# Seven products in place of eight for two output blocks of the last MLP's last pass, and a unit-wise activation in MLP 1

## The chip, the cores and the metric

The kernel runs on one core of a Trainium2 chip. The metric is device time in microseconds, the median of three runs. A core has TensorE (PE, matrix products into PSUM; PEld is its weight load), VectorE (DVE), ScalarE (ACT), GpSimd (POOL) and SyncE (SP, which issues the transfers from memory). Each engine works off its own queue of instructions in order.

## The reference

One sequence of 256 positions, width 2048, two layers: a short gated convolution with an MLP, then latent attention with an MLP. Behind each of the four sub-layers stands a normalisation of `ALPHA * x + f(x)`. The change is in the two MLPs:

```python
D_MODEL = 2048; SEQ = 256; D_FF = 4 * D_MODEL
ALPHA = (2 * DEPTH) ** 0.25

def sq_relu_mlp(x, w1, w2):
    return jnp.square(jax.nn.relu(x @ w1)) @ w2

h = layer_norm(ALPHA * h + mix, ln_g[layer, 0], ln_b[layer, 0])
h = layer_norm(ALPHA * h + sq_relu_mlp(h, mlp_w1[layer], mlp_w2[layer]), ln_g[layer, 1], ln_b[layer, 1])
```

All is float32.

## The kernel before, in words

*Two halves for each operand.* A float32 operand is split into a high part in a reduced format and a low part (`split`, L134: ScalarE casts the high part, L136, and VectorE subtracts it, L137). A product is then three matmuls: high by high, high by low, low by high. Weights come raw from memory in pieces of 128 x 1024 (512 KB, `load_raw`), and are split like this. `take` (L192) hands out the pieces in the order of the list `stream`, and has those prepared that lie up to five steps ahead. There are seven buffers for raw pieces and nine pairs for split ones.

*An MLP* (`mlp`, L586; `idx` 1 is MLP 1, `idx` 3 the last MLP) has 8192 hidden columns in eight passes (`q`, 0 to 7) of eight units (`m`, 0 to 7) of 128. A unit is a product with `w1`: 16 pairs of matmuls (`mm_run`, L230), a 512-wide one with the high part (L224) and a 256-wide one with the low part (L228). `turned=2` swaps the two at the third pair; `TURN` (L41) says for which units. The result is brought out of PSUM by `whole` (L363: ScalarE copies one half, L366, VectorE adds the other, L367), goes through relu and square (L732), and is split into `h` (tiles h1c, h1a in MLP 1; h3c, h3a in the last MLP). Two neighbouring units form a pair, and share one tile `u`.

*The way down.* The second product with `w2` has four output blocks of 512 columns, for two halves `t` of 128 rows each. In passes 0 and 7 it is done plainly (`down`, L324, `dot`, L306): for each block, half and unit three matmuls 512 wide. In passes 1 to 6 (`FAST`) two blocks at a time (`g` 0 or 1: blocks 0 and 1, or 2 and 3) take a pair of units as a 2 x 2 problem, by seven products in place of eight (`fast_products`, L356; `FACTORS`, L351). For that `form` (L641) makes three sums out of the pair, the pair's split grows to 896 columns, and a piece of `w2f` is prepared by `prepare` with three more sums (L171, L175, L178), three splits of 1024 and one of 512. The seven running results stand in seven PSUM banks; where the pair of blocks changes, they are put back (`put_back`, L620) into `acc` and `sums`, and the next are fetched (`resume`, L693). At the end `fold` (L622) adds them up, eight sums of 512 for each `g`, three or two behind each unit of pass 7. Products stand five units behind their own (`SHIFT`): pass 7 begins with products of pass 6.

*The end of MLP 1.* Pass 7's pair of units 6 and 7 goes through relu, square and split together. Then the four blocks follow by `down` in `to_wide` (L767). The residual, parked in memory, is fetched into the place of `sums` by POOL (L763), and VectorE scales it (L419).

*The end of the last MLP.* Pass 7's units 5 to 7 have no products between them. `last_sum` (L633) copies the folded blocks back into PSUM banks, `to_out` (L1026) adds all four blocks of pass 7 plainly on top: blocks 0 and 1 by `down`, then blocks 2 and 3 by `down_late`, half `t` = 0 ahead of `t` = 1. `finished` (L1041) takes statistics of each block (L1042), multiplies by the gain (L1045, for `t` = 1), and with the last block of a half normalises and stores: by VectorE for `t` = 0 (L1056, L1059), and for `t` = 1 partly by four matmuls (L1071, L1076) and a last step on ScalarE (L1080). The gains and offsets `gbt` are fetched in the place of the units' input, so behind the last unit.

*Order.* Within what the data allow a scheduler sets the order of each engine's queue when the kernel is built. `tc.issue_after(ins)` puts the instructions made inside it behind `ins` on `ins`'s engine.

The lines at the place of the stream that change:

```python
def mlp_stream(l):
    out = halves(w1[l, :QC]) + halves(w2[l, 0])
    for q, m, pair in steps():
        out += halves(w1[l, q * QC + m])
        if pair:
            p, i, j, g = pair
            out.append((w2f[l, p, g, j, 0], w2f[l, p, g, j, 1]))
    return out + halves(w2[l, NQ - 1])
```

Of the kernel before, what the change touches and what calls it, by code (L numbers as in the profile page):

```python
# [40 lines left out]
def TURN(q, m, extra):  # L41
    return m == 0 or not (q == 1 and m < SHIFT or q == NQ - 1 and m > SHIFT) or extra and q == 1 and m <= NB
# [14 lines left out]
def trunk(ctx: ExitStack, tc: tile.TileContext, xT, vecs, lead, w_first, w_in, w_out, w_kv, w_q, w_uk, w_uv,  # L57
# [31 lines left out]
    def steps():  # L89

        for q in range(1, NQ):
            for m in range(QC):
                p, i = (q, m - SHIFT) if m >= SHIFT else (q - 1, m + QC - SHIFT)
                yield q, m, (p, i // NB, i % NB, (p % 2) ^ (i // NB)) if p in FAST else None

    def mlp_stream(l):
        out = halves(w1[l, :QC]) + halves(w2[l, 0])
        for q, m, pair in steps():
            out += halves(w1[l, q * QC + m])
# [34 lines left out]
    def split(hi, lo, src):  # L134

        nc.scalar.copy(hi, src)  # L136
        nc.vector.tensor_tensor(lo, src, hi.bitcast(F32), ALU.subtract)  # L137
# [218 lines left out]
    def fast_products(ps, x, j, fresh, ready, onto=()):  # L356

        b, = take(1, 6)
        a = {n: [x[j // 2][:, j % 2, o, i * P:(i + 1) * P] for o in range(2)] for i, n in enumerate(LEFT)}
        for p, l, r in FACTORS:  # L360
            dot(ps[p], b[r], a[l], p in fresh, p in ready, onto=p in onto)
# [224 lines left out]
    def mlp(idx, ln, blocks, fast, begin=None, extra=None, last=False):  # L586
# [43 lines left out]

        finals = {}
# [50 lines left out]
        factors = [act.tile([P, QC // 4, 2, 7 * P], F32R, tag=tag, name=f"h{idx}{tag}") for tag in ("c", "a2")]  # L682
# [13 lines left out]
        begun = {0: FAST[0], 1: FAST[0]}  # L696

        def products_of(p, i, j, g):
# [12 lines left out]
            if p == FAST[-1] and j == NB - 1:  # L711
                folds = chain(folds, fold(g))

        for q, m, pair in steps():
# [11 lines left out]
            late = q in FAST and m >= QC - 2  # L726
# [6 lines left out]
            if m % 2 and (m > 1 or lone):  # L733
                finish_pair(m // 2, u)
# [8 lines left out]
            if q == NQ - 1:  # L743
                for _ in range(3 if m >= SHIFT else 2):
                    next(folds, None)
            if pair:
                products_of(*pair)
            if m == 1 and not lone:
                finish_pair(0, u)
# [276 lines left out]
    def to_out(block, finals, h):  # L1026
# [13 lines left out]

        def finished(n, t, ps):  # L1041
            nc.vector.bn_stats(out=stats[:, t, n, :], in_=ps)  # L1042
            if n < NB - 1:
# [18 lines left out]
            if t == 0:  # L1062
                rsqrt(r, ve)
                for i in range(NB):
# [5 lines left out]
            for i in range(n):  # L1070
                nc.tensor.matmul(finals[i, t], means, gbt[:, i, :BW], start=False, stop=i > 0, skip_group_check=True)  # L1071
# [4 lines left out]
            nc.tensor.matmul(finals[0, t], devs, gbt[:, 0, BW:], start=False, stop=True, skip_group_check=True)  # L1076
            scaled(n, us[n], gbt[:, n, BW:])
            for i in range(1, n):
                scaled(i, finals[i, t], gbt[:, i, BW:])
            nc.scalar.activation(block(0, t), finals[0, t], AF.Copy, scale=r)  # L1080
            store(t, 0)
# [102 lines left out]
```

## Time and profile before

| what | value |
|---|---|
| median of three runs | 2000.63 us (2000.51 to 2001.29) |
| the profiled execution's own time | 2002.59 us |
| its span | 2000.7 us |
| granted clock of TensorE, mean | 0.998 |
| moved from memory | 384 MB, 194 GB/s over the span |

In the profile a row of a timeline gives start, duration, engine, line, operation, tiles and shape, and in square brackets the idle time of the engine ahead of it with what ended it; `x2` means two in a row. In a row of a group stand the count, the busy time and the mean duration of one, then the idle time ahead of them. A row of a table of stretches gives from:to and length, then the busy time of each engine with its count of instructions, the granted clock, the share of the transfer engines and their rate. The end of a matmul is modelled, so the step from one matmul's start to the next one's says more than its duration; VectorE, too, starts an instruction a little ahead of the shown end of the one before.

### The profile page before, as it was taken

What the parts mean: (1) busy time and instruction counts of PE and PEld (TensorE: products, weight loads), DVE (VectorE), ACT (ScalarE), POOL (GpSimd) and SP (SyncE); (2) the same over time, 40 slices, a digit from 0 to 9 for tenths busy, and PEclk for the clock granted to TensorE, in tenths of its full rate; (3) what the DMA queues carried; (4) which work ended last, traced back from release to release, by engine and by line L of the source; (5) the groups of instructions that cost most, each with busy time, mean ns of one, the idle gap of its engine ahead of it and who ended that gap; (6) DMA issues with size and microseconds to landing.
All of it is one profiled execution on the core that took longest, in us unless ns stands there. A gap on an engine that the chain in (4) does not pass through costs nothing.

```text
span 2000.7 us, 29698 instructions
## 1 busy us (share of the span) xinstructions
PE 1988.5 (99%) x11062; PEld 1732.5 (87%) x11062; DVE 1720.3 (86%) x2505; ACT 1289.0 (64%) x1914; POOL 5.6 (0%) x27
## 2 busy tenths in 40 slices
PE   9999999999999999999999999999999999999998
PEld 8888888988788888888889998898888888888886
DVE  8667667787899999999988988778889999999995
ACT  6444445586667777677756665558666776767772
POOL 0000000000000000000000000000000000000000
PEclk9999999999999999999999999999999999999999
DMA  9766666574565555665764643656456556565572
GB/s 339 213 190 189 189 189 190 182 238 143 180 215 191 200 194 196 210 205 204 246 223 153 184 144 106 211 182 196 140 194 216 170 203 216 180 212 197 205 267 96
DMA packets 107712, 390.00 MB, mean 195 GB/s; under 512 B 11952, under 2 KB 12720, under 8 KB 107056
## 3 DMA queue, kind: packets, MB, share of 16 engines
q1 hardware_dynamic: 106560, 383.79, 58.7%
q0 software_dynamic: 864, 4.19, 0.6%
q8 instruction: 86, 1.41, 0.3%
q14 instruction: 58, 0.48, 0.1%
q10 hardware_dynamic: 144, 0.13, 0.0%
HBM read 383.87 MB, written 4.19 MB: 194 GB/s over the span
## 4 chain that ended last, share of the span: by engine, by line
PE 95%; DMA 2%; DVE 1%; issue 1%; ACT 0%; SPq 0%; DVEq 0%; POOLq 0%; ACTq 0%
PE ps_u L224 20%; PE ps_l L224 13%; PE ps_u L228 10%; PE ps L312 7%; PE ps L311 7%; PE ps L309 7%; PE ps_l L228 7%; PE ps_d L312 2%; PE ps_d L309 2%; PE ps_d L311 2%; PE ps_w L258 2%; PE ps_w L257 2%; PE ps_w L256 2%; DMA raw<-in_w2f_dram 1%; PE ps_g L258 1%; PE ps_g L256 1%
## 5 line engine op out<-in xcount | busy, mean ns | idle before, releaser
L137 DVE TENSOR_TENSOR lo<-raw,hi 128x1024 fp32r<-128x1024 f32 x710 | 854.6, 1218 | 167.1 <-ACT hi L136 97.6
L136 ACT CAST hi<-raw 128x1024 fp32r<-128x1024 f32 x710 | 732.5, 1054 | 220.2 <-PE ps_l L224 102.2
L224 PE MATMUL ps_u<-xhl,hi 128*128 128x512 f32 x1792 | 621.2, 393 | 0.0
L228 PE MATMUL ps_u<-xhl,lo 128*128 128x256 f32 x1792 | 485.0, 280 | 0.0
L224 PEld LDWEIGHTS ps_u<-xhl,hi 128*128 128x128 f32 x1792 | 328.8, 187 | 67.5 <-DVE fp L367 0.9
L228 PEld LDWEIGHTS ps_u<-xhl,lo 128*128 128x128 f32 x1792 | 338.1, 189 | 12.9
L224 PE MATMUL ps_l<-xhl_a,hi 128*128 128x512 f32 x704 | 244.1, 393 | 0.0
L228 PE MATMUL ps_l<-xhl_a,lo 128*128 128x256 f32 x704 | 195.4, 279 | 0.0
L136 ACT CAST hi_t<-raw_t 128x1024 fp32r<-128x1024 f32 x96 | 101.5, 1057 | 120.4 <-DVE raw_t L171 115.4
L224 PEld LDWEIGHTS ps_l<-xhl_a,hi 128*128 128x128 f32 x704 | 132.1, 188 | 29.9
L228 PEld LDWEIGHTS ps_l<-xhl_a,lo 128*128 128x128 f32 x704 | 131.9, 188 | 0.2
L171 DVE TENSOR_TENSOR raw_t<-raw,raw 128x1024 f32<-128x1024 f32 x96 | 116.9, 1217 | 9.8 <-DMA raw<-in_w2f_dram 9.8
L137 DVE TENSOR_TENSOR lo_t<-raw_t,hi_t 128x1024 fp32r<-128x1024 f32 x96 | 116.9, 1218 | 2.1 <-ACT hi_t L136 1.7
L366 ACT COPY t<-ps_u 128x256 f32<-128x256 f32 x112 | 41.7, 372 | 95.0 <-PE ps_u L228 94.7
L224 PE MATMUL ps_l<-z,hi 128*128 128x512 f32 x240 | 82.4, 391 | 0.0
L258 PE MATMUL ps_w<-xd,hi 128*128 128x258 f32 x256 | 72.7, 284 | 0.0
L256 PE MATMUL ps_w<-xd,hi 128*128 128x258 f32 x256 | 72.3, 282 | 0.0
L257 PE MATMUL ps_w<-xd,lo 128*128 128x258 f32 x256 | 72.3, 282 | 0.0
L224 PE MATMUL ps_l<-oT,hi 128*128 128x512 f32 x208 | 71.3, 391 | 0.0
L732 ACT ACTIVATE fp<-fp 128x512 f32<-128x512 f32 (+1 forms) x112 | 65.9, 588 | 7.2 <-DVE fp L367 6.8
L178 DVE TENSOR_TENSOR raw<-raw 128x512 f32<-128x512 f32 x96 | 66.1, 688 | 2.0
L175 DVE TENSOR_TENSOR raw<-raw,raw_t 128x512 f32<-128x512 f32 x96 | 65.6, 683 | 0.8
(350 smaller groups left out, 3880.0 us busy)
## 6 DMA issues: line engine op xcount, KB each, us to landing
raw<-in_w_dram SPq DMA_DIRECT2D x320, 512.0 KB, 4.1
raw<-in_w2f_dram SPq DMA_DIRECT2D x192, 512.0 KB, 5.2
raw<-in_w_in_dram SPq DMA_DIRECT2D x88, 512.0 KB, 3.7
raw<-in_w_out_dram SPq DMA_DIRECT2D x32, 512.0 KB, 3.7
raw<-in_w_o_dram SPq DMA_DIRECT2D x32, 512.0 KB, 4.2
raw<-in_w_kv_dram SPq DMA_DIRECT2D x10, 512.0 KB, 4.6
raw<-in_w_q_dram SPq DMA_DIRECT2D x8, 512.0 KB, 4.0
raw<-in_w_uk_dram SPq DMA_DIRECT2D x8, 512.0 KB, 4.6
```

What stands on the lines that cost most here:

```text
L136: nc.scalar.copy(hi, src)
L137: nc.vector.tensor_tensor(lo, src, hi.bitcast(F32), ALU.subtract)
L171: nc.vector.tensor_tensor(t.rearrange(two, a=2), b12.unsqueeze(1).to_broadcast([P, 2, BW]), r1.rearrange(two, a=2), ALU.subtract)
L178: nc.vector.tensor_tensor(t4, b21, b12, ALU.subtract)
L224: nc.tensor.matmul(ps, w[blk // 8][0][:, blk % 8, :], x, start=first, stop=False)
L228: nc.tensor.matmul(ps[:, :T], w[blk // 8][1][:, blk % 8, :], x[:, :T], start=False, stop=last)
L256: nc.tensor.matmul(ps[:, :W], hi, x[k][:, :W], start=k == 0, stop=False)
L257: nc.tensor.matmul(ps[:, :W], lo, x[k][:, :W], start=False, stop=False)
L258: nc.tensor.matmul(ps[:, :W], hi, x[k][:, W:], start=False, stop=k == NC - 1)
L309: nc.tensor.matmul(ps, x[0], w[0], start=first, stop=False, skip_group_check=onto)
L311: nc.tensor.matmul(ps[:, at], x[0], w[1][:, at], start=False, stop=False, skip_group_check=onto)
L312: nc.tensor.matmul(ps, x[1], w[0], start=False, stop=last, skip_group_check=onto)
```

## The change

For MLP 1: units 6 and 7 of pass 7 are activated and split each by itself; unit 6's square stays on ScalarE, unit 7's is done on VectorE in one instruction.

For the last MLP: pass 7's output blocks 2 and 3 are done by seven products. `steps` runs past pass 7 for that: the pairs 0 to 3 of pass 7 stand behind its units 5, 6, 7 and at the end. The products go on in the banks in which pass 6 left blocks 2 and 3; behind pair 3 four of the seven results (`OWN`) are put back into `sums`, three stay in PSUM. `last_sum` fetches blocks 0 and 1 alone. `down_late` then does blocks 0 and 1, and behind its first block stand (`between`) the eight sums of `fold_last`, some of them in PSUM, and the statistics of blocks 2 and 3. The order of the blocks in the normalisation is 2, 3, 0, 1. The instructions on VectorE that are made between pair 3's split and the end of the pass stand behind that split (`issue_after`). The factors' tiles grow from seven to eight columns of 128 and hold the pair's plain values, too. `TURN` loses the case for units 1 to 4 of the last MLP's pass 1, which stand behind transposes.

```diff
-def TURN(q, m, extra):
-    return m == 0 or not (q == 1 and m < SHIFT or q == NQ - 1 and m > SHIFT) or extra and q == 1 and m <= NB
+def TURN(q, m):
+    return m == 0 or not (q == 1 and m < SHIFT or q == NQ - 1 and m > SHIFT)
...
-    def steps():
+    def steps(last):
-        for q in range(1, NQ):
-            for m in range(QC):
+        for q in range(1, NQ + 1):
+            for m in range(QC if q < NQ else SHIFT):
                 p, i = (q, m - SHIFT) if m >= SHIFT else (q - 1, m + QC - SHIFT)
-                yield q, m, (p, i // NB, i % NB, (p % 2) ^ (i // NB)) if p in FAST else None
+                pair = (p, i // NB, i % NB, (p % 2) ^ (i // NB)) if p in FAST or last and p == NQ - 1 and i < NB else None
+                if q < NQ or pair:
+                    yield q, m, pair
...
-        return out + halves(w2[l, NQ - 1])
+        return out + halves(w2[l, NQ - 1, :2] if l else w2[l, NQ - 1])
...
-    def down_late(x, put, blocks, sums):
+    def down_late(x, put, blocks, sums, between):
         ws = {}
         for t in range(2):
             for n in blocks:
+                if t == 0 and n != blocks[0]:
+                    between()
...
+        def fold_last(g):
+            s1, s5, s7, s6 = (sums[:, i, g, :] for i in range(4))
+            left, right = 2 * g, 2 * g + 1
+            finals.update({(left, 1): ps["2"], (right, 1): ps["3"], (left, 0): ps["4"], (right, 0): block(right, 0)})
+            for d, a, b in ((ps["2"], ps["2"], s1), (s6, s6, s1), (ps["3"], ps["3"], s6), (s7, s7, s6),
+                            (ps["4"], ps["4"], s7), (block(right, 0), block(right, 0), s7), (ps["3"], ps["3"], s5),
+                            (block(right, 0), block(right, 0), s5)):
+                nc.vector.tensor_tensor(d, a, b, ALU.add)
...
         def finish_pair(j, u):
             f = factors[j // 2][:, j % 2]
-            if q in FAST:
+            if q in FAST or last:
                 form(u)
-                split(f[:, 0, :], f[:, 1, :], u[:, P:])
+                at = slice(P if q in FAST else 0, 8 * P)
             else:
-                split(f[:, 0, :2 * T], f[:, 1, :2 * T], u[:, :2 * T])
+                at = slice(0, 2 * T)
+            return split(f[:, 0, at], f[:, 1, at], u[:, at])
...
-        factors = [act.tile([P, QC // 4, 2, 7 * P], F32R, tag=tag, name=f"h{idx}{tag}") for tag in ("c", "a2")]
+        factors = [act.tile([P, QC // 4, 2, 8 * P], F32R, tag=tag, name=f"h{idx}{tag}") for tag in ("c", "a2")]
...
-            end = i == 0 or p == FAST[-1]
+            end = i == 0 or p == FAST[-1] and not last
...
                 for o in order:
+                    if p == NQ - 1:
+                        if o in OWN:
+                            put_back(o, g, ps[o])
+                        continue
                     put_back(o, g, ps[o])
...
-        for q, m, pair in steps():
+        for q, m, pair in steps(last):
             lone = pair is None
+            if q == NQ:
+                products_of(*pair)
+                if pair[2] == NB - 1:
+                    behind.close()
+                continue
...
-            at = "6" if lone and m % 2 == 0 else "unit"
+            at = "6" if lone and (m - SHIFT) % 2 else "unit"
             un = psum("ps_u", bank[at])
-            mm_run([(w, un)], xhl, 0, NC, NC, turned=TURNED if TURN(q, m, extra) else None)
+            mm_run([(w, un)], xhl, 0, NC, NC, turned=TURNED if TURN(q, m) else None)
...
-            late = q in FAST and m >= QC - 2
+            late = m >= QC - 2
...
-            if m % 2 and (m > 1 or lone):
-                finish_pair(m // 2, u)
+            if late and q not in FAST and not last:
+                f, at = factors[m // 4][:, 1], slice(m % 2 * T, (m % 2 + 1) * T)
+                split(f[:, 0, at], f[:, 1, at], u[:, at])
+            else:
+                rows[m // 2] = u
+            if m % 2 and (m > 1 or lone) and m // 2 in rows:
+                made = finish_pair(m // 2, rows.pop(m // 2))
+                if last and q == NQ - 1 and m == QC - 1:
+                    behind.enter_context(tc.issue_after(made.ins))
...
-                for _ in range(3 if m >= SHIFT else 2):
+                for _ in range(3 if m >= SHIFT else 2 if not last or m > 2 else 0):
...
-            if q == NQ - 1 and last and m >= QC - 2:
-                for t in range(2):
-                    last_sum(m - QC + 2, t, spare[2 * (m - QC + 2) + t])
...
-            for i, (n, t) in enumerate(((2, 0), (3, 0), (2, 1), (3, 1))):
-                last_sum(n, t, spare[4 + i])
-            blocks(block, finals, h)
+            for n, t, o in ((0, 0, "unit"), (1, 0, "1"), (0, 1, "5"), (1, 1, "7")):
+                last_sum(n, t, bank[o])
+            blocks(block, finals, h, lambda: fold_last(1))
...
+        order = (2, 3, 0, 1)
...
-            if n < NB - 1:
+            if n != order[-1]:
...
+            one = order[0]
+            for i in order[:-1]:
+                nc.tensor.matmul(finals[i, t], means, gbt[:, i, :BW], start=False, stop=i != one, skip_group_check=True)
...
-        for n in range(2):
-            down(h, finished, n, finals)
-        down_late(h, finished, range(2, NB), finals)
+        def between():
+            fold_last()
+            for t in range(2):
+                for n in order[:2]:
+                    finished(n, t, finals[n, t])
+
+        down_late(h, finished, order[2:], finals, between)
```

More of the change, by code (lines that the diff above doesn't have):

```diff
@@ L87, in trunk @@
     stream += halves(w_out)
-    def steps():
-        for q in range(1, NQ):
-            for m in range(QC):
+    def steps(last):
+        for q in range(1, NQ + 1):
+            for m in range(QC if q < NQ else SHIFT):
                 p, i = (q, m - SHIFT) if m >= SHIFT else (q - 1, m + QC - SHIFT)
-                yield q, m, (p, i // NB, i % NB, (p % 2) ^ (i // NB)) if p in FAST else None
+                pair = (p, i // NB, i % NB, (p % 2) ^ (i // NB)) if p in FAST or last and p == NQ - 1 and i < NB else None
+                if q < NQ or pair:
+                    yield q, m, pair
     def mlp_stream(l):
         out = halves(w1[l, :QC]) + halves(w2[l, 0])
-        for q, m, pair in steps():
-            out += halves(w1[l, q * QC + m])
+        for q, m, pair in steps(l == 1):
+            if q < NQ:
+                out += halves(w1[l, q * QC + m])
             if pair:
@@ L358, in fast_products @@
         b, = take(1, 6)
-        a = {n: [x[j // 2][:, j % 2, o, i * P:(i + 1) * P] for o in range(2)] for i, n in enumerate(LEFT)}
+        a = {n: [x[j // 2][:, j % 2, o, i * P:(i + 1) * P] for o in range(2)] for i, n in enumerate(LEFT, 1)}
         for p, l, r in FACTORS:
@@ L696, in mlp @@
         begun = {0: FAST[0], 1: FAST[0]}
+        rows = {}
+        behind = ExitStack()
         def products_of(p, i, j, g):
@@ L710, in products_of @@
                         resume(o, 1 - g)
-            if p == FAST[-1] and j == NB - 1:
+            if p == FAST[-1] and j == NB - 1 and end:
                 folds = chain(folds, fold(g))
-        for q, m, pair in steps():
+        for q, m, pair in steps(last):
             lone = pair is None
+            if q == NQ:
[3 more added lines that the diff above has]
+                continue
             if q == FAST[0] and m == SHIFT:
@@ L1024, in turn_residual, with to_out @@
         nc.vector.scalar_tensor_tensor(block(n, t), ps, ALPHA, block(n, t), ALU.mult, ALU.add)
-    def to_out(block, finals, h):
+    def to_out(block, finals, h, fold_last):
         gbt = act.tile([P, NB, 2 * BW], F32, tag="b", name="gbt")
@@ L1063, in finished @@
                 rsqrt(r, ve)
-                for i in range(NB):
+                for i in order:
                     centred(i)
@@ L1075, in finished @@
             nc.scalar.activation(devs, id_t, AF.Copy, scale=ve)
-            nc.tensor.matmul(finals[0, t], devs, gbt[:, 0, BW:], start=False, stop=True, skip_group_check=True)
+            nc.tensor.matmul(finals[one, t], devs, gbt[:, one, BW:], start=False, stop=True, skip_group_check=True)
             scaled(n, us[n], gbt[:, n, BW:])
-            for i in range(1, n):
+            for i in order[1:-1]:
                 scaled(i, finals[i, t], gbt[:, i, BW:])
-            nc.scalar.activation(block(0, t), finals[0, t], AF.Copy, scale=r)
-            store(t, 0)
-        for n in range(2):
-            down(h, finished, n, finals)
-        down_late(h, finished, range(2, NB), finals)
+            nc.scalar.activation(block(one, t), finals[one, t], AF.Copy, scale=r)
+            store(t, one)
+        def between():
[4 more added lines that the diff above has]
+        down_late(h, finished, order[2:], finals, between)
     with tc.tile_pool(name="fast2", bufs=1) as fast:
```

6 lines of the change are left out of this document (2 added, 4 removed).

## The prediction

> **What bounds the kernel now.** I read the page first, then the busy time by stretch, then three stretches in order of time.
>
> ```profile
> PE 1988.5 (99%) x11062; PEld 1732.5 (87%) x11062; DVE 1720.3 (86%) x2505; ACT 1289.0 (64%) x1914; POOL 5.6 (0%) x27
> ...
> PE 95%; DMA 2%; DVE 1%; issue 1%; ACT 0%; SPq 0%; DVEq 0%; POOLq 0%; ACTq 0%
> ...
> L136 ACT CAST hi<-raw 128x1024 fp32r<-128x1024 f32 x710 | 732.5, 1054 | 220.2 <-PE ps_l L224 102.2
> ```
>
> TensorE is busy 99% and holds 95% of the chain of waits, so each matmul taken out should count at its full price; but VectorE has 14% left over the whole kernel only. What it has left at the end, where the change works, is in the stretches:
>
> ```profile
> core 0: us, PE busy (x) PEld busy (x) DVE busy (x) ACT busy (x) POOL busy (x), PEclk, DMA share, GB/s
> 1901.10:1931.00 29.90, 29.90 (x155) 25.53 (x155) 29.90 (x36) 22.75 (x33) 0.00 (x0) 1.00 0.70 224
> 1931.00:1947.60 16.60, 16.60 (x98) 14.62 (x97) 16.29 (x21) 14.74 (x23) 0.00 (x0) 1.00 0.89 326
> 1947.60:1969.00 21.40, 21.40 (x97) 17.70 (x96) 12.84 (x14) 10.75 (x14) 0.00 (x0) 1.00 0.51 177
> 1969.00:1991.30 22.30, 22.28 (x99) 18.12 (x97) 10.62 (x22) 0.20 (x1) 0.00 (x0) 1.00 0.13 47
> ```
>
> TensorE is full in all four. VectorE is full until 1931 and nearly until 1947.6 (end of the last unit); its idle time is 0.0 + 0.3 + 8.6 + 11.7 = 20.6 us, nearly all in the plain products at the end. ScalarE has 7.2 + 1.9 + 10.7 = 19.7 us free before 1969.
>
> The end itself:
>
> ```profile
> 1947.56 0.39 PE L309 MATMUL ps_e<-hi,h3c 128*128 128x512 f32 x1
> ...
> 1990.90 0.39 PE L312 MATMUL ps_e<-hi,h3a 128*128 128x512 f32 x1
> ...
> 1991.32 0.70 DVE L1042 BATCH_NORM_STATS2 stats<-ps_e 128x6 f32<-128x512 f32 x1 [2.81 <-PE ps_e L312]
> ...
> 1996.60 0.69 ACT L1080 ACTIVATE acc<-ps_e,rr 128x512 f32<-128x512 f32 x1 [1.90 <-PE ps_e L1076]
> ```
>
> The 192 matmuls of the last four blocks start 0.227 us apart (43.34 us over 191). The last statistics begin as soon as the last matmul is out, and 9.4 us of normalisation and stores follow to the end of the span at 2000.7. VectorE had waited 2.81 us there: TensorE sets the end.
>
> **The change part by part.** *MLP 1's last pass.* Between its last unit and its first output block the profile has a stall:
>
> ```profile
> 1009.74 0.29 DVE L419 TENSOR_SCALAR xback<-xback 128x256 f32<-128x256 f32 x1 [5.11 <-DMA xback<-parked]
> ...
> 1009.95 1.22 DVE L137 TENSOR_TENSOR lo<-raw,hi 128x1024 fp32r<-128x1024 f32 x1
> ...
> 1010.23 0.39 PE L311 MATMUL ps_d<-lo,h1a 128*128 128x512 f32 x1
> 1011.09 0.68 DVE L137 TENSOR_TENSOR h1a<-fp,h1a 128x512 fp32r<-128x512 f32 x1
> ...
> 1011.82 0.50 PE L312 MATMUL ps_d<-hi,h1a 128*128 128x512 f32 x1 [1.20 <-DVE h1a L137]
> ```
>
> L312 is the first matmul that needs the low half of the last pair. That half stands on VectorE behind L419, which waited 5.11 us for the residual coming back by DMA. TensorE's step is 1.59 us instead of 0.23, and the first matmul behind it is 0.1 longer: 1.5 in all. After the change unit 6 has a split of its own, which the new order puts ahead of L419; unit 7's split stays behind it. So TensorE goes on at 1010.46 with six matmuls that need nothing of unit 7's low half (L312 and a triple of unit 6, L309 and L311 of unit 7) and asks for it at 1010.46 + 6 x 0.23 = 1011.84. Unit 7's split, now 256 wide, starts at 1011.09 as before and ends near 1011.5. The stall goes: **-1.5** (bounds -1.5 and 0, if the DMA lands later). The added half-width square on VectorE runs inside its 5.11 us of waiting. What could be late next are the weight splits behind it: they move up 0.3 us and TensorE 1.5. They are the third block's, two blocks of 48 matmuls (11 us each) ahead; without that cover up to 1.2 would come back.
>
> *TURN for units 1 to 4 of MLP 2's second pass.* These units follow eight transposes and lose their turned order.
>
> ```profile
> 458.34 0.39 PE L224 MATMUL ps_u<-xhl,hi 128*128 128x512 f32 x1
> ...
> 463.89 0.39 PE L224 MATMUL ps_u<-xhl,hi 128*128 128x512 f32 x1
> ...
> 475.73 0.47 PE L224 MATMUL ps_u<-xhl,hi 128*128 128x512 f32 x1
> ...
> 481.44 0.40 PE L224 MATMUL ps_u<-xhl,hi 128*128 128x512 f32 x1
> ...
> 1406.71 0.47 PE L224 MATMUL ps_u<-xhl,hi 128*128 128x512 f32 x1
> ...
> 1412.36 0.38 PE L1023 MATMUL turned<-id_t,xback 128*128 128x128 f32 x2
> ```
>
> From first to next first matmul: 5.55 for an unturned unit behind a unit, 5.71 for an unturned one behind other matmuls, 5.65 turned behind transposes. Per unit the loss lies between 5.71 - 5.65 = 0.06 and, if transposes count as a unit does, 5.55 + 0.08 (the longer first step) - 5.65 = -0.02. Nearest is the 5.71 (other matmuls in front): 4 x 0.06, **+0.2** (bounds -0.1 and +0.3). Units 6 and 7 of the last pass now stand behind products without a turn, about 0.1 each; the stall found below covers that.
>
> *The seven products.* Blocks 2 and 3 took 2 blocks x 2 row halves x 8 units x 3 = 96 matmuls and take 4 pairs x 7 products x 3 = 84: 12 x 0.227 = -2.7 on TensorE. For this VectorE pays. Starts of consecutive rows give the price of one:
>
> ```profile
> 1877.60 0.28 DVE L645 TENSOR_TENSOR fp<-fp 128x128 f32<-128x128 f32 x1
> 1877.80 1.21 DVE L137 TENSOR_TENSOR lo<-raw,hi 128x1024 fp32r<-128x1024 f32 x1
> 1878.93 0.41 DVE L646 TENSOR_TENSOR fp<-fp 128x256 f32<-128x256 f32 x1
> 1879.27 0.68 DVE L178 TENSOR_TENSOR raw<-raw 128x512 f32<-128x512 f32 x1
> ...
> 1904.39 0.68 DVE L137 TENSOR_TENSOR h3c<-fp,h3c 128x512 fp32r<-128x512 f32 x1
> ...
> 1907.27 1.22 DVE L171 TENSOR_TENSOR raw_t<-raw,raw 128x1024 f32<-128x1024 f32 x1
> 1908.40 0.41 DVE L367 TENSOR_TENSOR fp<-ps_u,t 128x256 f32<-128x256 f32 x1
> 1908.74 0.68 DVE L628 TENSOR_TENSOR sums<-sums 128x512 f32<-128x512 f32 x1
> 1909.34 0.68 DVE L175 TENSOR_TENSOR raw<-raw,raw_t 128x512 f32<-128x512 f32 x1
> ```
>
> 1.13 us for 1024 wide, 0.60 for 512, 0.34 for 256, 0.20 for 128. Each of the four pairs adds on VectorE two of 1024 (L171 and one more split), three of 512 (L175, L178, the seventh factor's split), the three sums of *form* (0.20 + 0.34 + 0.20), and its own split grows from 512 to 1024: 2.26 + 1.80 + 0.74 + 0.53 = 5.3, and 21.5 with the four, 0.3 more for the last square. The sixteen fold sums stay sixteen; eight are moved behind the last unit. So **21.8 us of added work meet 20.6 us of idle time**: even if VectorE never waited again, the last statistics could start no earlier than 1991.32 + 1.2. The 2.7 cannot reach the end.
>
> It will wait, too. The first changed place of its queue is 1904.39. From there to the last sum of the last pair's *form* stand 37 of 1024, 23 of 512, seven of 256 and four sets of form: 41.8 + 13.8 + 2.4 + 3.0 = 61.0, so 1965.4; with some 0.8 of short waits (an estimate: the four *form* chains, where a sum waits for the one ahead of it, and splits right behind their casts) 1966.2. ScalarE's cast (1.05, the page's row) makes the operand ready at 1967.4. TensorE wants it earlier: without a stall its last dot would be over at 1991.1 - 2.7 = 1988.4 (0.3 later by the two unturned units), and 110 matmuls stand from the last pair's first product to that end, 25.0 us: 1963.7. It stalls about 3.7 us, parts of it at the first products of block 0, whose weight splits share that queue; the dots end near 1992.4 instead of 1991.1. VectorE meanwhile waits 1.2 for the cast, since the edge behind the last split (issue_after) holds back five weight splits, the folds and the statistics, and about 0.5 later for block 0's and block 1's ends. Last statistics: 1.2 + 1.2 + 0.5 = **+2.9**, at 1994.2, with TensorE done. The chain behind it keeps its length. Bounds: 0 (should the busy shares count 1.2 us of hand-over as work, and no wait come) and +5.3, with the clock's 2.4 below.
>
> *Without a price.* ScalarE's added casts, 4 x (1.05 + 0.5 + 0.5) = 8 us, fit its 19.7; without that room they would add to the cast's wait. SP issues the same sixteen transfers of 512 KB in the same place ahead of gbt, eight of them from the other weight array. POOL's queue is unchanged.
>
> Sum: -1.5 + 0.2 + 2.9 = +1.6. The profiled execution took 2002.59 (span 2000.7), so 2004.2 with a profile; the median runs 2.0 below it, so **2002.2**.
>
> **The rivals.** *The clock drops.* The profile has such a case at 518:
>
> ```profile
> 518.83 0.39 PE L311 MATMUL ps<-lo,h1a 128*128 128x512 f32 x1
> 521.39 0.79 PE L312 MATMUL ps<-hi,h1a 128*128 128x512 f32 x1 [2.18 <-DVE h1a L137]
> 521.99 0.63 PE L309 MATMUL ps<-hi,h1a 128*128 128x512 f32 x1
> ...
> 526.68 0.61 PE L312 MATMUL ps<-hi,h1a 128*128 128x512 f32 x1
> 527.11 0.42 PE L309 MATMUL ps<-hi,h1a 128*128 128x512 f32 x1
> ```
>
> After a stall of 2.2 (0.7 just before) eleven matmuls start 0.43 apart instead of 0.23: 11 x 0.20 and 0.2 at the first, 2.4. The stall at 1010 (1.2) had no such tail. My 3.7 us falls in pieces of 0.8, 2.2 and 0.7, much like 518; the statistics of block 0 wait for TensorE, so VectorE passes it on. Some of it covers the wait for the cast: +0.8 to +2.4, near 2004.0.
>
> The Trainium skill (TensorE: Matmul & The Clock Gate, Part 1) puts the drop behind an idle window of about 3.4 us; taken strictly the pieces would not do and 2002.2 stands, but at 518 two matmuls lay inside such a window and the clock dropped.
>
> *A late transfer (the slower side).* The last two weight halves follow four gbt transfers on SP:
>
> ```profile
> 1947.75 1.75 SPq L1029 DMA_DIRECT2D gbt<-in_gb_dram  x4
> 1949.61 1.79 SPq L147 DMA_DIRECT2D raw<-in_w_dram  x2
> ```
>
> Their issue now waits for the splits near 1964 to 1966. Were they to land past 1978, the folds behind their splits slip; at 3 us late, 2005. They have some 10 us, so this is unlikely. *MLP 1's stall stays* because its DMA lands later: 2003.7. *All fits* (the 2.7 reaches the end): 1996.6; against it stands the 21.8 in 20.6.
>
> **How the numbers follow.** Forecast 0.45 (own range 2001 to 2003.4), clock drop 0.33, late transfer 0.10, MLP 1 stays 0.07, all fits 0.05. I take 0.2%, 4 us, as what a measurement here can tell: slower means over 2004.6. That takes nearly half of the clock drop (0.15), the late transfer (0.09), a little of MLP 1: 0.25. Faster, under 1996.6, is most of all fits: 0.04. The rest, 0.71, is no change. The range reaches from no cost at the end (1999.1) to a late transfer's side of the clock drop (2005.3).
>
> **What would show it.** No step over 0.3 us on TensorE at MLP 1's first output block; four units of 5.7 behind the transposes; VectorE without idle time to the last form, then TensorE waiting for it and for ScalarE's cast of h3a; the last statistics some 3 us behind the last dot's wait, with VectorE busy ahead of it. Wrong I am if VectorE has idle time ahead of the last pair, or if its last statistics wait for TensorE again.

## The result, and the profile after

The changed kernel takes 2005.05 us (median of eleven, 2001.91 to 2006.52) against 2000.64 for the kernel before on the same chip (1997.86 to 2002.31): a ratio of 1.0021 (95% interval 1.0011 to 1.0030). It is 4.4 us slower. The profiled execution took 2003.71, its span 2001.9.

The page of the profile after, busy time by engine and the chain of waits by engine:

```profile
PE 1987.5 (99%) x11050; PEld 1732.0 (87%) x11050; DVE 1742.7 (87%) x2540; ACT 1292.1 (65%) x1916; POOL 5.6 (0%) x27
...
PE 98%; DVE 1%; DMA 0%; issue 0%; ACT 0%; DVEq 0%
```

VectorE has grown by 22.4 us (1720.3 before), close to the added work of the prediction, 21.8. TensorE has lost only 1.0. The last stage by stretches, with the clock granted to TensorE behind the busy times:

```profile
core 0: us, PE busy (x) PEld busy (x) DVE busy (x) ACT busy (x) POOL busy (x), PEclk, DMA share, GB/s
1897.10:1927.00 29.90, 29.90 (x155) 25.42 (x155) 29.90 (x38) 18.42 (x24) 0.00 (x0) 1.00 0.61 191
1927.00:1954.70 27.70, 27.70 (x145) 23.61 (x144) 27.66 (x35) 17.61 (x23) 0.00 (x0) 1.00 0.55 179
1954.70:1964.50 9.80, 7.26 (x26) 5.32 (x25) 8.39 (x13) 8.32 (x11) 0.00 (x0) 0.84 0.70 206
1964.50:1989.20 24.70, 24.70 (x109) 20.38 (x108) 23.04 (x38) 7.60 (x12) 0.00 (x0) 0.99 0.34 126
1989.20:2001.90 12.70, 5.62 (x10) 2.08 (x8) 6.38 (x14) 1.88 (x5) 0.00 (x0) 0.87 0.45 165
```

VectorE is full up to 1954.7, and in the 34.5 us from there to the last product it has 1.4 + 1.7 = 3.1 us free, where the whole stage had 20.6 before. TensorE waits in the third stretch and in the last, and in both its clock is under 1. First the third, TensorE's own rows:

```profile
1958.72 0.51 PE L312 MATMUL ps_e<-hi,h3c 128*128 128x512 f32 x1 [0.40 <-ACT hi L139]
1961.36 0.73 PE L314 MATMUL ps_e<-lo,h3c 128*128 128x512 f32 x1 [2.14 <-DVE lo L140]
1961.89 0.63 PE L315 MATMUL ps_e<-hi,h3c 128*128 128x512 f32 x1
...
1964.45 0.59 PE L314 MATMUL ps<-lo,h3a 128*128 128x512 f32 x1
1964.88 0.39 PE L312 MATMUL ps<-hi,h3a 128*128 128x512 f32 x1
```

The scheduler has put block 0's first matmuls (ps_e) ahead of the last pair's. They wait 2.14 us for a weight half from VectorE's full queue; then the clock is half, and matmuls start 0.43 us apart until 1964.9. Now VectorE around the last statistics, and TensorE behind the last product (1989.20):

```profile
1963.41 1.23 DVE L140 TENSOR_TENSOR h3a<-fp,h3a 128x1024 fp32r<-128x1024 f32 x1 [1.11 <-ACT h3a L139]
...
1984.19 0.70 DVE L1075 BATCH_NORM_STATS2 stats<-ps_e 128x6 f32<-128x512 f32 x1 [0.46 <-PE ps_e L315]
...
1988.36 2.73 DVE L1092 SCALAR_TENSOR_TENSOR acc<-u,rr,gbt 128x512 f32<-128x512 f32 x4
1991.01 0.70 DVE L1075 BATCH_NORM_STATS2 stats<-ps_e 128x6 f32<-128x512 f32 x1
```

```profile
1989.20 0.39 PE L315 MATMUL ps_e<-hi,h3a 128*128 128x512 f32 x1
1992.49 3.51 PE L1105 MATMUL ps<-gbt,umeans 128*128 128x512 f32 x4 [2.90 <-ACT umeans L1102]
```

The last statistics wait no more for TensorE (2.81 us before): VectorE is busy from 1984.19 on without a gap for 6.8 us, nearly all of it the normalisation of row half 0. TensorE idles 2.90 us, and the four closing matmuls then take 3.51 us where the same ones at full clock take 1.98 (a run below shows them).

In MLP 1 the stall has gone. VectorE's rows there:

```profile
1004.95 0.29 DVE L424 TENSOR_SCALAR xback<-xback 128x256 f32<-128x256 f32 x1 [2.81 <-DMA xback<-parked]
1005.15 1.22 DVE L140 TENSOR_TENSOR lo<-raw,hi 128x1024 fp32r<-128x1024 f32 x1
1006.29 0.42 DVE L140 TENSOR_TENSOR h1a<-fp,h1a 128x256 fp32r<-128x256 f32 x1
```

The last unit's split is 256 wide and done at 1006.7; TensorE's matmuls around it start 0.23 apart throughout.

To compare profiles whose earlier parts differ by some microseconds, I use three marks: the first matmul of the normalisation behind MLP 1 (tile ps_g; 1049.97 before, 1045.60 after), the last statistics, and ScalarE's last scaling.

| profile | ps_g to last statistics | last statistics to last scaling (the closing) |
|---|---|---|
| before | 941.35 | 5.28 |
| after | 945.41 (+4.06) | 6.74 (+1.46) |

### The profile page after: what moved, and what is told of

It reads as the page before. It is cut to its first block, busy times and chain, and to the rows that moved or that the text cites. A ratio compares the mean times of both kernels' runs of the same rounds, so it can differ in the third digit from the quotient of the medians.

```text
span 2001.9 us, 29701 instructions
## 1 busy us (share of the span) xinstructions
PE 1987.5 (99%) x11050; PEld 1732.0 (87%) x11050; DVE 1742.7 (87%) x2540; ACT 1292.1 (65%) x1916; POOL 5.6 (0%) x27
## 4 chain that ended last, share of the span: by engine, by line
PE 98%; DVE 1%; DMA 0%; issue 0%; ACT 0%; DVEq 0%
PE ps_u L227 20%; PE ps_l L227 13%; PE ps_u L231 11%; PE ps L315 8%; PE ps L314 8%; PE ps L312 8%; PE ps_l L231 7%; PE ps_d L315 2%; PE ps_d L314 2%; PE ps_d L312 2%; PE ps_w L261 2%; PE ps_w L260 2%; PE ps_w L259 2%; PE ps_g L261 1%; PE ps_g L259 1%; PE ps_g L260 1%
## 5 line engine op out<-in xcount | busy, mean ns | idle before, releaser
L139 ACT CAST hi_t<-raw_t 128x1024 fp32r<-128x1024 f32 x100 | 105.6, 1056 | 130.3 <-DVE raw_t L174 125.3
L174 DVE TENSOR_TENSOR raw_t<-raw,raw 128x1024 f32<-128x1024 f32 x100 | 122.2, 1222 | 9.3 <-DMA raw<-in_w2f_dram 9.2
L140 DVE TENSOR_TENSOR lo_t<-raw_t,hi_t 128x1024 fp32r<-128x1024 f32 x100 | 122.0, 1220 | 1.9 <-ACT hi_t L139 1.4
L140 DVE TENSOR_TENSOR t<-raw,t 128x512 fp32r<-128x512 f32 x100 | 68.7, 687 | 0.0
```

Source lines behind the costliest of these rows:

```text
L140: return nc.vector.tensor_tensor(lo, src, hi.bitcast(F32), ALU.subtract)
L174: nc.vector.tensor_tensor(t.rearrange(two, a=2), b12.unsqueeze(1).to_broadcast([P, 2, BW]), r1.rearrange(two, a=2), ALU.subtract)
```

## The experiments

Times are medians; ratios are to the kernel before on the same chip, with 95% intervals. Eleven executions each, except where told.

### MLP 1's part alone

```diff
-            late = q in FAST and m >= QC - 2
+            late = m >= QC - 2 and (q in FAST or not last)
...
+            if late and q not in FAST:
+                f, at = factors[m // 4][:, 1], slice(m % 2 * T, (m % 2 + 1) * T)
+                split(f[:, 0, at], f[:, 1, at], u[:, at])
```

> The kernel before with MLP 1's part of the change alone (last pair of its last pass activated and split unit by unit). Theory (the stall at 1010 goes and nothing comes back): 1.5 us less than before, about 1999.1, ratio 0.9993; no step over 0.3 us on TensorE at MLP 1's first output block, last stage as before (99.6 us from unit 0's product at 1901 to the end of the span). Rival (the gain is given back in the normalisation behind MLP 1): 2000.6, ratio 1.000.

1999.35 against 2000.59, ratio 0.9994 (0.9985 to 1.0003); from ps_g to the last statistics 941.34, the closing 5.28, both as before. No step of TensorE is over 0.25 us longer than usual in MLP 1's last blocks. The gain of 1.2 agrees with the 1.5 and is not given back, though the interval by itself would allow none.

### The end alone

The changed kernel with `late` as before in MLP 1 and `TURN` as before.

> The changed kernel without MLP 1's part and with the old turned order for units 1 to 4. Theory (the whole cost is in the last stage, 5.2 us longer in the profiles): about 2006, ratio 1.0027; the units behind the transposes take 5.65 us as before. Rival 1 (most of the loss comes from the shift in time that MLP 1's part makes, which moves the drops of the clock): 2000.6 to 2002. Rival 2 (the lost turned order costs 0.2 us): its units are 0.06 us shorter each than the changed kernel's 5.63 to 5.74.

2005.94 against 2000.59, ratio 1.0025 (1.0016 to 1.0034): the whole loss and more. TensorE and VectorE at the end:

```profile
1959.83 0.50 PE L312 MATMUL ps_e<-hi,h3c 128*128 128x512 f32 x1 [0.40 <-ACT hi L139]
1962.47 0.50 PE L314 MATMUL ps_e<-lo,h3c 128*128 128x512 f32 x1 [2.14 <-DVE lo L140]
1964.53 0.50 PE L312 MATMUL ps<-hi,h3a 128*128 128x512 f32 x1 [0.42 <-ACT h3a L139]
```

```profile
1991.24 0.69 DVE L1075 BATCH_NORM_STATS2 stats<-ps_e 128x6 f32<-128x512 f32 x1
```

```profile
1992.72 3.78 PE L1105 MATMUL ps<-gbt,umeans 128*128 128x512 f32 x4 [2.90 <-ACT umeans L1102]
```

The same stall of 2.14 has no half clock behind it here. From ps_g to the last statistics it takes 944.19, **+2.84**: that is the case without a drop, for which the prediction had +2.9. The closing takes 8.17, +2.89, with its fp32 matmuls at half clock (3.78 us for four).

The old turned units behind the transposes take 5.65 us each (5648, 5648, 5648, 5645 ns), the changed kernel's 5636, 5739, 5626, 5629, and the unit behind them takes 5.56 in the changed kernel instead of 5.63: together nothing, and not +0.2.

### Filling matmuls behind the last product

```diff
+            busy(finals[order[0], 0], 12)
             means = scratch("means")[:, :P]
```

`busy` makes so many matmuls of 128x512 into a bank that nobody reads any more.

> The changed kernel with twelve matmuls more behind the last output product, into a bank that nobody reads any more, so that TensorE is busy for some 2.7 us of the 3.3 us before the closing fp32 matmuls. Theory (the clock halves because TensorE idles there, and that makes the closing chain 1.5 us longer): 1.5 us less than the changed kernel, about 2003.5; closing matmuls at 0.43 us each instead of 0.62 to 1.0. Rival (the closing matmuls are slow for another reason, or the drop comes whatever TensorE does): the changed kernel's time, plus up to 0.3 for the added matmuls.

2002.68, ratio 1.0010 (1.0001 to 1.0018), some 2.2 us under the changed kernel's 1.0021, more than the 1.5 expected from one profile. The two intervals overlap, so the size is uncertain; that the closing grows shorter is in the rows. TensorE's closing:

```profile
1987.88 2.88 PE L793 MATMUL ps<-h3c 128*128 128x512 f32 x12
1990.94 1.98 PE L1111 MATMUL ps<-gbt,umeans 128*128 128x512 f32 x4 [0.18 <-ACT umeans L1108]
```

Work that computes nothing makes the kernel faster. The closing is 5.22 again; from ps_g to the last statistics it is still 945.06 (+3.71), with the half clock near 1960.

### The eight fold additions left out

```diff
-            if p == FAST[-1] and j == NB - 1 and end:
+            if p == FAST[-1] and j == NB - 1 and end and not last:
```

> The changed kernel without the eight fold additions of output blocks 0 and 1 on VectorE (4.8 us of its queue ahead of the last pair's operand); those blocks lack their shared products. Theory (VectorE's queue sets the end): the last pair's operand comes 4.8 us earlier, TensorE's stall and half clock near 1960 go, the last statistics stand some 5 us earlier and wait for TensorE again; 4 to 6 us less than the changed kernel, 1999 to 2001. Rival 1 (the half clock by itself is the loss, the queue is not): 0.8 to 1.7 less. Rival 2 (the last weight halves arrive late by DMA and set the end): within 0.5 of the changed kernel.

2000.48, ratio 0.9999 (0.9991 to 1.0008), 4.4 by ratios under the changed kernel. This profile has no half clock at the end, so part of the 4.4 is the clock; the stretch from ps_g is 942.15, +0.80, so 3.3 less than after, of which the drop near 1960 is 0.87 (below). Relief in VectorE's queue ends TensorE's stall (its longest step there is 0.77 us, where it was 2.64), so that queue is its cause. But the last statistics still do not wait for TensorE:

```profile
1971.57 0.70 DVE L1075 BATCH_NORM_STATS2 stats<-ps_e 128x6 f32<-128x512 f32 x1 [0.27 <-PE ps_e L315]
...
1981.75 0.26 DVE L1081 BATCH_NORM_AGGREGATE mv<-stats 128x2 f32<-128x24 f32 x1
1982.48 0.70 DVE L1075 BATCH_NORM_STATS2 stats<-ps_e 128x6 f32<-128x512 f32 x1 [0.46 <-PE ps_e L315]
...
1986.65 2.73 DVE L1092 SCALAR_TENSOR_TENSOR acc<-u,rr,gbt 128x512 f32<-128x512 f32 x4
1989.30 0.69 DVE L1075 BATCH_NORM_STATS2 stats<-ps_e 128x6 f32<-128x512 f32 x1
```

That is why +0.80 is left, though 4.8 us were taken away. From 1971.57 (block 0, row half 0) on VectorE waits only once more for TensorE, 0.46 us at 1982.48 (block 0, row half 1), and needs 17.7 us to the last statistics. TensorE has 72 matmuls left at that point, 16.3 us by 0.227 each, and starts the last at 1987.49. The changed kernel has the same 17.7 (1973.29 to 1991.01). That is a second, shorter path through VectorE. Row half 0's own statistics are complete at 1981.75 (the aggregate), but its normalisation stands in the queue behind the statistics that wait until 1982.48.

### Two scalings moved behind the last statistics

```diff
-                for i in order:
-                    centred(i)
-                    scaled(i, us[i], gbt[:, i, BW:])
+                for i in order:
+                    centred(i)
+                for i in order[:2]:
+                    scaled(i, us[i], gbt[:, i, BW:])
+                rest.extend(lambda i=i: scaled(i, us[i], gbt[:, i, BW:]) for i in order[2:])
...
+            with tc.issue_after(scaled(n, us[n], gbt[:, n, BW:]).ins):
+                for late in rest:
+                    late()
```

> The changed kernel with two of the four scalings of row half 0 (L1092, 0.66 us each) moved on VectorE behind the last statistics and row half 1's first scaling, where VectorE waits for TensorE. Theory (the last statistics stand behind the 6.8 us of normalisation of row half 0, which cannot begin before block 1's first row half ends, 5.0 us ahead of the last product): last statistics 1.3 us earlier; TensorE idle 2.0 instead of 3.3 us ahead of the closing matmuls, too short for the clock to halve there: 1.3 to 3 us less than the changed kernel, 2002 to 2003.7. Rival (the weight splits and folds in VectorE's queue ahead of 1984 set the last statistics): no change, 2005.

2003.56, ratio 1.0016 (1.0007 to 1.0025). The last statistics follow the last product by 0.48 us (1.81 in the changed kernel), and TensorE, now idle for 1.57, keeps its clock:

```profile
1990.62 0.39 PE L315 MATMUL ps_e<-hi,h3a 128*128 128x512 f32 x1
1992.58 1.98 PE L1109 MATMUL ps<-gbt,umeans 128*128 128x512 f32 x4 [1.57 <-ACT umeans L1106]
```

So the work of VectorE behind block 0, with the normalisation of row half 0 as its end, is what holds the last statistics: 16.4 us instead of 17.7 (1974.69 to 1991.10). The expectation had its start wrong, for here too the aggregate of row half 0 (1984.88) stands ahead of the statistics that wait (1985.61). The time gained, 1.0 by ratios (whose intervals overlap) to 1.5 by medians, is at the lower edge of what was expected: in this profile the span ends 5.4 us behind the start of ScalarE's last scaling instead of 4.1, and another run (the last one below) has that without the moved scalings. Why the last store takes longer there stays open.

### The additions on GpSimd

```diff
-                nc.vector.tensor_tensor(d, a, b, ALU.add)
+                (nc.gpsimd if last else nc.vector).tensor_tensor(d, a, b, ALU.add)
```

> The changed kernel with the eight fold additions of blocks 0 and 1 on GpSimd instead of VectorE. Theory (VectorE's queue delays the last pair and the first weight halves): as with the additions left out, 2000.5; TensorE's stall of 2.1 us near 1960 goes. Rival (GpSimd's additions slow VectorE's or come too late for row half 0's products): VectorE's operations in that stretch grow longer, 2002 to 2006.

2008.59, ratio 1.0043 (1.0031 to 1.0056; five executions): worse even than the rival's 2002 to 2006. GpSimd's additions, and VectorE beside them:

```profile
1890.11 1.63 POOL L633 TENSOR_TENSOR acc<-acc,sums 128x512 f32<-128x512 f32 x1 [883.37 <-ACT acc L625]
1891.70 1.30 POOL L633 TENSOR_TENSOR sums<-sums 128x512 f32<-128x512 f32 x1
1893.07 2.33 POOL L633 TENSOR_TENSOR acc<-acc,sums 128x512 f32<-128x512 f32 x1
```

```profile
1893.01 1.23 DVE L140 TENSOR_TENSOR lo<-raw,hi 128x1024 fp32r<-128x1024 f32 x1 [2.43 <-ACT hi L139]
1894.48 2.00 DVE L140 TENSOR_TENSOR lo<-raw,hi 128x1024 fp32r<-128x1024 f32 x1 [0.24 <-ACT hi L139]
1896.41 2.31 DVE L140 TENSOR_TENSOR lo_t<-raw_t,hi_t 128x1024 fp32r<-128x1024 f32 x1
```

While GpSimd adds, VectorE's splits take 2.0 to 2.3 us instead of 1.22. TensorE waits 1.35 us for VectorE at 1899 and 1.64 at 1914. With both moves together:

> Both, the additions on GpSimd and the two scalings moved. Theory: 2000.5 less 1.3, so 1999.2, under the kernel before (2000.6) and level with MLP 1's part alone (1999.4). Rival (the two gains are the same wait counted twice): no better than the better of the two alone.

2006.00, ratio 1.0032 (1.0020 to 1.0044; six executions). A miss: 1999.2 was expected. The moved scalings give 2.6 on top of the additions on GpSimd, and those cost more than that. Part of both is the clock: from ps_g to the last statistics the two profiles have +6.37 and +4.95, but the closing takes 8.25, with a half clock, in the first and 5.21 in the second.

### The clock by itself

```python
for e in range(GAPS):
    burst = 34 + (e * 7) % 17
    ps = pmm.tile([P, BW], F32, tag="ps", name="ps")
    for k in range(burst):
        nc.tensor.matmul(ps, a, x, start=k == 0, stop=k == burst - 1)
    ...
    nc.vector.tensor_scalar(x, src, 1.0 / burst, None, ALU.mult)
```

> No part of the reference (the output is zeros): 120 bursts of 34 to 50 matmuls of 128x512 (0.23 us each) with idle gaps of some 0.8 to 5 us between, made by chains of VectorE operations. Theory (drawn from the six profiles so far: the clock is set by windows of 3.41 us on a fixed grid, and is half in the window that follows one with TensorE busy less than about 0.4 of it): all drops begin at multiples of 3.413 us from one another; a window with a busy share under 0.37 is followed by a half one, one over 0.43 is not; gaps of 2.1 to 3.4 us drop the clock sometimes, by their place on the grid, longer ones always, shorter ones never. Rival (the drop follows the length of one idle time): one length parts the gaps with a drop from those without, wherever they lie.

One execution. Two neighbouring windows, the second of them half, and the one ahead of both:

```profile
1345.68:1349.09 3.41, 3.41 (x17) 2.76 (x15) 0.00 (x0) 0.00 (x0) 1.00 0.00 0
1349.09:1352.51 3.42, 1.09 (x5) 0.67 (x4) 2.08 (x7) 0.00 (x0) 1.00 0.00 0
1352.53:1355.94 3.41, 3.41 (x10) 2.63 (x9) 0.00 (x0) 0.00 (x0) 0.50 0.00 0
```

There are 50 drops, 53 half windows. All begin at whole multiples of 3.4133 us from one another, within 3 ns. Taking each matmul's step (up to 0.232 us) as busy, the windows at full clock divide like this:

```
busy share of the window   next at half   next at full
under 0.385                     41              0
0.385 to 0.425                   8              8
over 0.425                       0            330
```

The parting line is near 0.40 (the highest share with a drop behind it is 0.41, the lowest without one 0.39). In a window that is itself half, the busy time counts by half: three with 0.31, 0.33 and 0.38 stay half, all from 0.40 on go back to full. The rival falls: of twenty gaps of 2.4 to 2.5 us ten had a drop and ten none.

That tells the two stalls of 2.14 us apart. The windows of the changed kernel, then of the kernel with the end alone:

```profile
1958.04:1961.46 3.42, 0.88 (x4) 0.29 (x2) 3.42 (x5) 3.04 (x4) 0.00 (x0) 1.00 0.63 168
1961.46:1964.87 3.41, 3.41 (x8) 2.66 (x9) 2.23 (x5) 2.54 (x3) 0.00 (x0) 0.50 0.76 196
```

```profile
1957.73:1961.15 3.42, 2.20 (x9) 1.26 (x7) 3.42 (x5) 3.42 (x6) 0.00 (x0) 1.00 0.50 196
1961.15:1964.56 3.41, 1.67 (x7) 1.08 (x7) 2.23 (x6) 2.17 (x4) 0.00 (x0) 1.00 0.71 226
```

In the first the stall lies inside one window (share 0.13 by steps; the row's busy time also counts the modelled ends of matmuls), in the second it is cut in two (0.52 and 0.41). The 0.41 lies in the band where half of the windows had a drop behind them; that none came here fits the rule, but is not forced by it. The price of the drop is seen from the last unit's last product to the last statistics: 36.39 us with it, 35.52 without, 0.87.

### The stall in MLP 1's second pass, filled

The kernel before has a drop of its own at 518 (the prediction's row), and so have nearly all profiles. The first try was MLP 1's part alone with six matmuls in front of what I took for the waiting pair:

> The kernel before with MLP 1's part of the change alone, and six matmuls more (1.4 us) on a bank that the next product clears, in front of the first pair of seven products in MLP 1, where TensorE waits 0.6 and 2.3 us near 518. Theory (the clock halves when TensorE is busy less than 0.40 of a fixed window of 3.41 us): TensorE is idle at most 1.5 us there, so no window falls under 0.40, the half clock at 520 (seen in five of six profiles, 1.5 to 2.9 us long in its effect) goes; 1.2 to 2 us less than MLP 1's part alone, near 1997.8, and no half clock before the last stores. Rival (TensorE's wait is what costs, the clock adds nothing that VectorE does not hide): 1999.4.

2000.40 against 2001.16, ratio 0.9996 (0.9987 to 1.0005): the six ran at 533, where nothing waits, and the half clock at 520 stayed. A miss of the place, not of the rule. The same six with all three fills on the changed kernel:

> The changed kernel with filling matmuls at all three places where its clock halves: the six near 518, twelve with a zero operand ahead of the last pair's products near 1958, the twelve behind the last product. Theory (the change itself costs 2.8 us by VectorE's queue, the rest of its loss is the clock): no half clock in the kernel before its last stores; 2.8 us more than MLP 1's part with its six filling matmuls, so near 2000.6, which is 4 us less than the changed kernel. Rival 1 (without the drops the shorter TensorE work comes through): level with that kernel, near 1998. Rival 2 (the drops move to other places): 2003 or more.

2003.22, ratio 1.0006 (0.9997 to 1.0015), 2.8 over its companion by medians, 2.0 by ratios; from ps_g 944.20 (+2.85). The two drops at the end are gone, the one at 520 is not. Then MLP 1's part alone with eight at the right place:

```diff
+            if p == FAST[0] and i == 0 and j == NB - 1 and not last:
+                for _ in range(8):
+                    nc.tensor.matmul(ps["3"], zero[:, :P], xhl[0], start=False, stop=False, skip_group_check=True)
```

> As the run with six filling matmuls before, but with eight (1.8 us), with a zero operand, at the place where TensorE does wait: ahead of the fourth pair's products in MLP 1, near 517 (the six had gone to 533, where nothing waits). Theory (half clock after a window with TensorE busy less than 0.40): TensorE's idle time near 518 shrinks from 2.9 to some 1.1 us, the window's busy share stays above 0.5, no half clock at 520; 1.5 us less than MLP 1's part alone where that has the drop, median near 0.9987 of the kernel before, nearly all executions with a mean clock of 1.000. Rival (as with the six: the fill only adds work): 0.9995 of the kernel before or more.

```profile
517.11 2.01 PE L704 MATMUL ps<-xhl,zero 128*128 128x512 f32 x8
518.96 0.39 PE L309 MATMUL ps<-hi,h1a 128*128 128x512 f32 x1
519.19 0.39 PE L311 MATMUL ps<-lo,h1a 128*128 128x512 f32 x1
520.12 0.50 PE L312 MATMUL ps<-hi,h1a 128*128 128x512 f32 x1 [0.55 <-DVE h1a L137]
```

1997.64 against 2001.52, ratio **0.9981** (0.9972 to 0.9990): faster than both kernels, and 2.6 by ratios under MLP 1's part alone: more than the 1.5 expected. Two half windows in a row, like those in the profile of before, cost 2.4, but the profile of MLP 1's part alone has one; the two intervals overlap and hold 1.5 as well. All eleven executions have a mean clock of 1.000 and lie within 2.4 us. At last the changed kernel with the three fills in their right places:

> The changed kernel with filling matmuls at the three places where its clock halves, the one near 518 where TensorE does wait (eight), the other two as in the run with all three before. Theory (without the clock's drops the change at the end costs 2.8 us by VectorE's queue): no half clock before the last stores; 2.8 us more than MLP 1's part with its eight filling matmuls (0.9981 of the kernel before), so 0.9995, with all executions at a mean clock of 1.000. Rival (what is left of the loss is clock or chance): level with that kernel, 0.998.

2000.86 against 2001.18, ratio 0.9995 (0.9986 to 1.0004), as expected, 2.8 by ratios over the run before it; the two intervals overlap, so the size is better known from the profile: from ps_g 943.93 (+2.58), the closing 5.22, no half clock ahead of 1997. Not all executions have a clock of 1.000: four of eleven show 0.999, the profiled one among them, whose only half window lies under the last stores.

## Why the prediction was right or wrong

**The time, 2002.2, was 2.9 too low, inside its range.** That it lies inside is partly luck: the upper end, 2005.3, was set by a late transfer with a clock drop, and the time came near it by a drop in the closing that the prediction did not have. The likeliest case was wrong: its +2.9 came, and on top of it the rival's clock drop and a second drop that no case had.

- *MLP 1, -1.5:* right. -1.2 alone, and no stall in the profile.
- *TURN, +0.2:* nothing. The lower bound's reason was the true one: transposes count as a unit does. Only a size was off.
- *VectorE's 21.8 into 20.6, +2.9 at the last statistics:* +2.84 in the one profile with no drop on the way, +2.85 and +2.58 with the drops filled. The details hold too: VectorE waits 1.11 us for the cast (1.2 predicted) and 0.27 + 0.48 for two blocks' ends (0.5). Counted on the time axis of before (2.92 added), the profile of the end alone has the cast of the last pair ready at 1967.4 (predicted 1967.4), its last product at 1992.35 (near 1992.4) and the last statistics at 1994.16 (1994.2). That the stall and 3.3 us of the stretch (0.87 of them the clock's) go with VectorE work left out shows the cause; that filling TensorE's waits leaves 2.6 to 2.8 standing shows that it is no matter of the clock. What I did not see is how the last 1.3 is bound: behind block 0's first row half VectorE has 17.7 us to go where TensorE has 16.3, whatever happened in the queue in front. (The prices of the prediction's list add up to 5.33 a pair, 21.6 in all instead of 21.8; nothing hangs on that.)
- *"The chain behind it keeps its length":* this is the step that failed. The matmuls of that chain had waited 1.6 us before; with the last statistics 1.8 behind the start of the last product instead of 0.4, TensorE waits 2.9, and in the profile after the clock halves under the closing matmuls: +1.46, with the end alone +2.89, 2.2 on the median. Here, too, the place on the grid decides: with the fold additions left out TensorE waits 2.89 at the same place, and the four matmuls behind it take 1.98 us, at full clock. I looked for the drop in the stall that I had found, and not in the wait that the same delay makes at the end. It follows from the sum itself: products end near 1992.4, last statistics at 1994.2.
- *The rival of the clock drop, 0.33, +0.8 to +2.4:* it came, in three of four profiles that keep the stall (after, the closing filled, the scalings moved; not with the end alone), at 0.87, the low end.
- *By the Trainium skill's rule* (TensorE: Matmul & The Clock Gate, Part 1) an idle window of about 3.4 us was needed, and 2002.2 would stand. Measured are drops after windows up to 0.41 busy, so some 2 us without work inside one window are enough. Where the Trainium skill says there that the window runs freely at 3413 ns, the run by itself agrees.
- *A late transfer, MLP 1 stays, all fits:* did not come. The last weight halves did wait for their transfer (ScalarE's cast by 1.93 us at 1972.9), but TensorE starts a matmul every 0.23 us from 1964.9 to the last product, so that wait does not set the end.

The account on medians: -1.2 (MLP 1) + 2.8 (VectorE) + 2.2 (closing) + 0.87 in those executions in which the drop near 1960 falls so. That is 3.8 to 4.7; measured 4.4.

The chances were too mild: slower by over 0.2% had 0.25, for the clock was put in one place only.

## What to carry to other kernels

A new wait of the engine that sets the end is to be priced twice, by its length and by what it does to the clock; and each delay is to be followed to every later place where the same engine waits. Where more than about 2 us of waiting on TensorE can't be removed, a few matmuls that compute nothing can pay, at the very place in its queue where it waits: 1.4 us of added matmuls at a wrong place did nothing, 1.8 at the right one gave 2.6. Taking work off the engine with the full chain pays only if the engine that takes over has room in the stretch where the work falls.

## What the runs showed of the hardware that I had not expected

- The clock of TensorE goes by windows of 3.413 us on a grid that does not follow the program (the edge ahead of the stall lies 3.4 us behind the start of the last unit's last product in the changed kernel, 2.0 with the end alone): half in the window behind one that was busy under 0.40, at half clock counted by half. So one kernel has the same stall with and without a drop, and executions of one program spread over 4 us and more: with a mean clock of 1.000 the kernel before lies between 1998.5 and 2000.3, with 0.998 between 2000.5 and 2003.6.
- GpSimd's additions of 128x512 take 1.3 to 2.3 us, and VectorE's 1024-wide subtractions beside them 2.0 to 2.3 instead of 1.22. The Trainium skill (SBUF — State Buffer, SBUF: two separate sides) tells of a port pair that the two share; the rows agree.
- The end of the span follows the start of ScalarE's last scaling by 4.1 to 4.5 us in most profiles and by 5.4 to 5.9 in three (both with moved scalings, and the changed kernel with the three fills in their right places). What parts them was not tried.
